# Banded attention scores: the low key parts in zero-padded tiles of full height

## Chip, cores and metric

The kernel runs on one NeuronCore of a Trainium2 chip. The metric is the device time of one execution in microseconds (us). The engines are named as in the profile: PE is TensorE's matrix multiply and PEld its weight load, DVE is VectorE, ACT is ScalarE, POOL is GpSimd, SP issues most DMAs.

## The reference, cut to what matters

One layer of a bidirectional hybrid encoder over 512 tokens of width 1024: a state space branch and a windowed attention branch side by side, a gated merge, cross attention to 256 memory rows, a feed-forward block. All is float32. The change lies in the windowed attention. It has 16 query heads of 64 features over 4 key heads; a block of 128 queries sees the key block before it, its own and the one after it.

```python
def windowed_gqa_with_sink(q, k, v, sink):
    ...
    qb = q.reshape(b, nb, ATTN_BLOCK, ATTN_KV_HEADS, ATTN_GQA, ATTN_HEAD_DIM)
    kb = band_blocks(k)
    vb = band_blocks(v)
    scores = jnp.einsum('bnqhrd,bnkhd->bnhrqk', qb, kb).astype(jnp.float32) * (ATTN_HEAD_DIM ** -0.5)
    ...
    scores = jnp.where(valid[None, :, None, None], scores, -jnp.inf)
    ...
    probs = jax.nn.softmax(jnp.concatenate([scores, sink_col], axis=-1), axis=-1)[..., :-1]
    out = jnp.einsum('bnhrqk,bnkhd->bnqhrd', probs.astype(v.dtype), vb)
    return out.reshape(b, s, ATTN_WIDTH)
```

## The kernel before

**Exact products in two parts.** Every float32 operand of a large product is split into a high part of the narrower type float32r and a low part, the rest. A projection (`mac`, lines 138 to 140) is then three matmuls for each 128 rows of the contraction: high by high, low activations by high weights, high activations by low weights. Weights come in granules of 128 x 1024; `load` fetches one (`raw`), ACT or DVE casts the high part (`whi`, lines 126 and 128), DVE or POOL subtracts to get the low part (`wlo`, line 129). Granules are prepared two steps ahead, in three buffers.

**The scores.** A query head has 64 features, and the PE contracts over up to 128 rows. `q_step` puts a head's high parts in one half of the 128 rows of its tile `qs` and the low parts in the other half. `k_step` puts the high key parts twice, in both halves of `kd`. One matmul (line 772) of the whole `qs` tile with `kd` therefore gives high by high plus low by high. The product of the high query parts with the low key parts is added by a second matmul (line 774), which takes only the 64 rows of `qs` that hold the high parts, and the same 64 rows of `kl`. Of `kl` there is one slot per pair of key heads: the low parts of one head fill its upper 64 rows, those of the other its lower 64.

**A block of attention.** `soft(pr, qb, kk)` handles four query heads that share a key head, for 128 queries; there are 16 such blocks, numbered 0 to 15 in this text in the order of execution. With 2 or 3 key blocks in reach a score row has 256 columns (blocks 0, 1, 6 to 9, 14, 15) or 384. For each head there is a pair of matmuls (lines 772 and 774) into one of two PSUM banks `sa`, then DVE's reduction (line 776), which adds the mask, finds the maximum and so frees the bank. After four of them three small DVE operations make the exponent's bias `ngm` (lines 780 to 782), ACT takes four exponentials (line 785), DVE adds and inverts the sums (787, 788) and normalises the four tiles (line 790). `turn` transposes the probabilities on PE (line 800), ACT copies them out (line 802), `mix` multiplies them by the values (line 813), ACT and DVE split the result (817, 818). The tiles `sm` have two buffers for each head, so the reductions of a block wait for the transposes of the block two before it.

**What sets the order.** `weave` spreads the attention steps among projection steps, and the framework then orders the instructions of each engine by its own estimates when the kernel is built; each engine runs its own list strictly in order. PE's list has projection matmuls between the score pairs one by one.

Of the kernel before, what the change touches and what calls it, by code (L numbers as in the profile page):

```python
# [9 lines left out]
F32 = mybir.dt.float32  # L10
F32R = mybir.dt.float32r
AF = mybir.ActivationFunctionType
ALU = mybir.AluOpType
AX = mybir.AxisListType

P = 128
D = 1024
S = 512
KT = D // P
NCH = S // P  # L20
# [8 lines left out]

# columns of the packed constants  # L30
C_ID, C_ONE = 0, 128
C_TRF, C_TRB = 256, 384
C_COS, C_SIN, C_MASK = 512, 1024, 1536
C_N = 1920
# columns of the packed vectors
V_MIX, V_XAT, V_MEM, V_FFN, V_FIN = 0, 8, 16, 24, 32
V_CW, V_CB, V_SSD = 40, 160, 184
V_DTB, V_AL, V_DSK, V_SNK = 200, 201, 202, 218
V_N = 234
# granules of the input projection  # L40
G_DT, G_K, G_V, G_Q, G_GA, G_SSD, G_GS, G_N = 0, 1, 3, 5, 13, 21, 61, 69
# [24 lines left out]
def weave(a, b):  # L66
    """The steps of a and b in one list, both spread evenly over it."""
    key = [((i + 0.5) / len(a), 0, i) for i in range(len(a))] + [((i + 0.5) / len(b), 1, i) for i in range(len(b))]
    return [(a, b)[w][i] for _, w, i in sorted(key)]
# [3 lines left out]
def bidir_hybrid_layer(ctx: ExitStack, tc: tile.TileContext, io, dbg=None):  # L73
    nc = tc.nc
# [11 lines left out]
    x1 = xp.tile([P, KT, S], F32, tag="x1", name="x1")  # L86
# [14 lines left out]

# [1 line left out]
    vec = const.tile([P, V_N], F32, tag="vec", name="vec")  # L103
# [4 lines left out]
    half = const.tile([P, 4], F32, tag="half", name="half")  # L108
# [4 lines left out]

# [1 line left out]
    def load(spec, i):  # L115
# [30 lines left out]

# [1 line left out]
    def rms_stat(pool, sumsq, nchunk, width, eps):  # L148
# [38 lines left out]
    def gain_split(hi, lo, t, g):  # L187
        """hi + lo = t * g, exactly split."""
        nc.scalar.activation(hi, t, AF.Copy, scale=g)
        nc.vector.scalar_tensor_tensor(lo, t, g, hi.bitcast(F32), op0=ALU.mult, op1=ALU.subtract)  # L190

# [1 line left out]
    steps = []  # L193
    st = {}
# [19 lines left out]

    # ======================= keys and values of the memory =======================
    # (in buffers that the state space branch uses later)
    opens("mp")
# [62 lines left out]
    def load_x():  # L280
        p = st["mp"]
        st["hh"] = p.tile([P, KT, S], F32R, tag="hh", name="hh")
        st["hl"] = p.tile([P, KT, S], F32R, tag="hl", name="hl")
        for nm in ("nb", "wt", "dec"):
            st[nm] = p.tile([P, NCH, 64], F32, tag=nm, name=nm)
        st["xacc"] = st["sp"].tile([P, S], F32, tag="vrow", name="vrow")
# [40 lines left out]

    # ======================= state space branch =======================
    def ssd_open():
# [5 lines left out]

    # time steps: softplus, cumulative sums within chunks, decays
    # (x1 is free until the first group is projected: it holds the intermediate values)
    def dt_step(w):
# [147 lines left out]
    def group_scan(g):  # L486
        # what each chunk receives from the chunks before (after) it
        def weigh(d, n):
# [21 lines left out]

        # cumulative decays of one head, both directions, the same row on every partition
        def rows(h):
# [39 lines left out]

        # within the chunks, two heads side by side: features of a head, by tokens
        def inner(i):
# [9 lines left out]

        # what arrives from other chunks, likewise
        def arrive(i):
# [20 lines left out]

        # gate with silu(z), kept doubled: the norm removes the factor
        def gate(i):
# [16 lines left out]
        nn, ar, ga, gs = ([w(i) for i in range(4)] for w in (inner, arrive, gather, gate))  # L606
        # stages of the heads: each stage some steps behind the one before
        order = []
# [34 lines left out]

    # first gates of this branch, while the last group is scanned
    def early_gate(m):
# [45 lines left out]

    # ======================= windowed attention =======================
    def at_open():
        p = st["at"]
        ca = p.tile([P, C_N - C_COS], F32, tag="ca", name="ca")
        nc.scalar.dma_start(ca, io["consts"][:, C_COS:C_N])
        st["ca"] = ca
        st["kd"] = p.tile([P, 4, S], F32R, tag="kd", name="kd")
        st["kl"] = p.tile([P, 2, S], F32R, tag="kl", name="kl")
        st["vt"] = p.tile([P, NCH, 256], F32, tag="vtok", name="vtok")  # L700
        st["oh"] = st["mo"].tile([P, KT, S], F32R, tag="oh", name="oh")
        st["ol"] = st["mo"].tile([P, KT, S], F32R, tag="ol", name="ol")
# [14 lines left out]
    def k_step(i):  # L717
        def f(w):
            t = rope(w)
            kd, kl = st["kd"], st["kl"]  # L720
            for kk in range(2):
                own, oth = slice(64 * kk, 64 * kk + 64), slice(64 - 64 * kk, 128 - 64 * kk)
                nc.scalar.copy(kd[own, 2 * i + kk], t[own])
                nc.scalar.copy(kd[oth, 2 * i + kk], t[own])
                nc.vector.tensor_tensor(kl[own, i], t[own], kd[own, 2 * i + kk].bitcast(F32), op=ALU.subtract)
        return f
# [17 lines left out]

    # q of one head: high parts over 64 partitions, low parts over the other 64
    def q_step(i):
# [13 lines left out]
    def soft(pr, qb, kk):  # L760
        def f():
            aw = st["at"]
            b0, b1 = blocks(qb)
            n = (b1 - b0) * P
            m0 = 2 * S + (b0 - qb + 1) * P
            own = slice(64 * kk, 64 * kk + 64)
            sm = [aw.tile([P, 384], F32, tag=f"sm{r}", name=f"sm{r}", bufs=2) for r in range(4)]
            mx, ngm, es, dn = (aw.tile([P, 4], F32, tag=t, name=t, bufs=2) for t in ("mx", "ngm", "es", "dn"))
            for r in range(4):
                sp = bank("sa")  # L770
                qs = st["qs", 4 * pr + r, kk]
                nc.tensor.matmul(sp[:, :n], qs[:, qb * P:(qb + 1) * P], st["kd"][:, 2 * pr + kk, b0 * P:b1 * P],  # L772
                                 start=True, stop=False)
                nc.tensor.matmul(sp[:, :n], qs[own, qb * P:(qb + 1) * P], st["kl"][own, pr, b0 * P:b1 * P],  # L774
                                 start=False, stop=True)
                nc.vector.tensor_tensor_reduce(
                    out=sm[r][:, :n], in0=sp[:, :n], in1=st["ca"][:, m0:m0 + n],
                    scale=1.0, scalar=-3.0e38, op0=ALU.add, op1=ALU.max, accum_out=mx[:, r:r + 1])
            snk = vec[:, V_SNK + 8 * pr + 4 * kk:V_SNK + 8 * pr + 4 * kk + 4]
            nc.vector.scalar_tensor_tensor(ngm, mx, 0.125, snk, op0=ALU.mult, op1=ALU.max)  # L780
            nc.vector.tensor_tensor(es, snk, ngm, op=ALU.subtract)
            nc.vector.tensor_scalar(ngm, ngm, -1.0, None, op0=ALU.mult)
            nc.scalar.activation(es, es, AF.Exp)
            for r in range(4):
                nc.scalar.activation(sm[r][:, :n], sm[r][:, :n], AF.Exp, bias=ngm[:, r:r + 1], scale=0.125,
                                     accum_out=dn[:, r:r + 1])
            nc.vector.tensor_tensor(dn, dn, es, op=ALU.add)
            nc.vector.reciprocal(dn, dn)
            for r in range(4):
                nc.vector.tensor_scalar(sm[r][:, :n], sm[r][:, :n], dn[:, r:r + 1], None, op0=ALU.mult)  # L790
            st["sm", kk] = sm
        return f
# [61 lines left out]

    # ======================= merge and output projection =======================
    def gate_a(m):
# [16 lines left out]

    # new residual tile, its split for the next projection, its square
    def residual(m, old, acc, gbase, sq):
# [27 lines left out]

    # ======================= cross attention =======================
    opens("xa")

    # keys and values of one head, split
    def kv_part(h):
# [104 lines left out]

    # ======================= feed forward =======================
    opens("ff")
# [43 lines left out]

    # last output tile and final norm, one half of the tokens after the other  # L1060
    def ff_last(*ws):
# [52 lines left out]

# [1 line left out]
    specs = [g for _, gr in steps for g in gr]  # L1116
# [26 lines left out]
def _gran(w):  # L1143
    """[K, M] -> [M/128, 128, K]: per output tile, the K tiles side by side."""
    k, m = w.shape
    return np.ascontiguousarray(w.reshape(k // P, P, m // P, P).transpose(2, 1, 0, 3)).reshape(m // P, P, k)
# [74 lines left out]
```

## Time and profile before

| | |
|---|---|
| median of 3 runs | 1351.72 us (1351.01 to 1351.82) |
| span of the profiled execution | 1350.6 us |
| PE busy | 1284.6 us, 95% of the span |
| DVE busy | 812.4 us, 60% |
| ACT busy | 580.8 us, 43% |
| first score matmul to the last | 604.0 to 725.5 us |

The profile gives the profiled execution by its span, from the first to the last instruction; its own time is not listed apart. The runs are timed from outside and lie 0.4 to 1.2 us above that span. Matmuls are pipelined and their listed ends are modelled: a PE that is listed as busy can still be waiting between two matmuls, so the starts of successive matmuls say what one costs.

### The profile page before, as it was taken

What the parts mean: (1) busy time and instruction counts of PE and PEld (TensorE: products, weight loads), DVE (VectorE), ACT (ScalarE), POOL (GpSimd) and SP (SyncE); (2) the same over time, 40 slices, a digit from 0 to 9 for tenths busy, and PEclk for the clock granted to TensorE, in tenths of its full rate; (3) what the DMA queues carried; (4) which work ended last, traced back from release to release, by engine and by line L of the source; (5) the groups of instructions that cost most, each with busy time, mean ns of one, the idle gap of its engine ahead of it and who ended that gap; (6) DMA issues with size and microseconds to landing.
All of it is one profiled execution on the core that took longest, in us unless ns stands there. A gap on an engine that the chain in (4) does not pass through costs nothing.

```text
span 1350.6 us, 16359 instructions
## 1 busy us (share of the span) xinstructions
PE 1284.6 (95%) x6084; PEld 1022.9 (76%) x6084; DVE 812.4 (60%) x1355; ACT 580.8 (43%) x1001; POOL 316.5 (23%) x259
## 2 busy tenths in 40 slices
PE   6889998998999999999999999999999999999996
PEld 5667776776777678876656888888888888888886
DVE  5797788788679776577765444566443444333323
ACT  6437376257256253256855333444332332222221
POOL 3344254234453562320000001100211111110001
PEclk9999999998999999999999999999999999999998
DMA  7435344243223323321102332411323322233331
GB/s 244 129 102 160 112 143 129 74 125 125 69 94 119 109 74 99 115 80 46 47 16 85 118 94 94 156 63 49 101 88 105 96 94 94 96 102 90 99 98 63
DMA packets 45440, 134.95 MB, mean 100 GB/s; under 512 B 5104, under 2 KB 8560, under 8 KB 45360
## 3 DMA queue, kind: packets, MB, share of 16 engines
q1 hardware_dynamic: 43072, 129.77, 30.4%
q10 hardware_dynamic: 1584, 2.03, 0.5%
q0 software_dynamic: 704, 2.10, 0.4%
q8 instruction: 48, 0.79, 0.2%
q14 instruction: 32, 0.26, 0.1%
HBM read 129.55 MB, written 4.33 MB: 99 GB/s over the span
## 4 chain that ended last, share of the span: by engine, by line
PE 69%; DVE 12%; issue 6%; POOL 6%; ACT 4%; DMA 2%; SPq 0%; DVEq 0%; POOLq 0%; ACTq 0%
PE mm L138 19%; PE mm L140 19%; PE mm L139 19%; DVE cvu L411 2%; DVE rt L538 2%; DVE wlo L129 2%; PE sa L774 2%; PE sb L813 2%; PE sb L800 1%; POOL mt L545 1%; POOL vv L585 1%; PE sa L772 1%; PE sb L986 1%; ACT whi L128 1%; PE sb L500 1%
## 5 line engine op out<-in xcount | busy, mean ns | idle before, releaser
L138 PE MATMUL mm<-hh,whi 128*128 128x512 f32 x968 | 388.4, 401 | 8.8 <-DVE cvu L411 5.4
L128 ACT CAST whi<-raw 128x1024 fp32r<-128x1024 f32 (+2 forms) x192 | 199.0, 1037 | 454.4 <-PE mm L139 394.0
L140 PE MATMUL mm<-hh,wlo 128*128 128x512 f32 x968 | 383.5, 397 | 0.9 <-DVE wlo L129 0.8
L139 PE MATMUL mm<-hl,whi 128*128 128x512 f32 x968 | 382.5, 395 | 0.2 <-DVE hl L310 0.2
L129 DVE TENSOR_TENSOR wlo<-raw,whi 128x1024 fp32r<-128x1024 f32 (+2 forms) x193 | 242.4, 1257 | 127.4 <-ACT whi L128 121.1
L138 PEld LDWEIGHTS mm<-hh,whi 128*128 128x128 f32 x968 | 184.8, 191 | 52.1 <-issue 10.3
L140 PEld LDWEIGHTS mm<-hh,wlo 128*128 128x128 f32 x968 | 184.2, 190 | 43.1 <-issue 2.3
L139 PEld LDWEIGHTS mm<-hl,whi 128*128 128x128 f32 x968 | 184.5, 191 | 39.0 <-issue 1.6
L185 POOL TENSOR_TENSOR sq_acc<-sq_acc,sq 128x512 f32<-128x512 f32 x14 | 24.8, 1771 | 276.4 <-ACT sq L184 276.4
L1039 POOL TENSOR_TENSOR fa<-fa,row 128x512 f32<-128x512 f32 x22 | 39.1, 1779 | 192.3 <-ACT fa L1038 192.3
L411 DVE SCALAR_TENSOR_TENSOR cvu<-mm,hcw,cvu 128x510 f32<-128x510 f32 (+1 forms) x96 | 70.9, 739 | 5.9 <-ACT cvu L408 5.5
L138 PE MATMUL mm<-fh,whi 128*128 128x512 f32 (+1 forms) x198 | 72.4, 366 | 0.0
L139 PE MATMUL mm<-fl,whi 128*128 128x512 f32 (+1 forms) x198 | 72.4, 365 | 0.0
L140 PE MATMUL mm<-fh,wlo 128*128 128x512 f32 (+1 forms) x198 | 72.4, 365 | 0.0
L138 PE MATMUL mm<-vh,whi 128*128 128x512 f32 (+1 forms) x192 | 71.5, 373 | 0.0
L140 PE MATMUL mm<-vh,wlo 128*128 128x512 f32 (+1 forms) x192 | 69.3, 361 | 0.0
L139 PE MATMUL mm<-vl,whi 128*128 128x512 f32 (+1 forms) x192 | 68.8, 358 | 0.0
L538 DVE TENSOR_SCALAR rt<-rt,nb 128x128 f32<-128x128 f32 x128 | 52.5, 466 | 20.9 <-POOL rt L530 17.5
L545 POOL TENSOR_TENSOR mt<-rt 128x512 f32<-128x512 f32 x32 | 48.0, 1503 | 71.8 <-ACT rt L539 33.8
L1041 DVE TENSOR_TENSOR ft<-fa,mm 128x512 f32<-128x512 f32 x22 | 15.1, 688 | 72.8 <-PE mm L140 70.7
L528 ACT ACTIVATE ear<-rt 64x1024 f32<-64x1024 f32 x32 | 33.9, 1060 | 55.7 <-POOL vv L585 51.9
L140 PE MATMUL mm<-oh,wlo 128*128 128x512 f32 x128 | 50.2, 392 | 0.0
(233 smaller groups left out, 2070.3 us busy)
## 6 DMA issues: line engine op xcount, KB each, us to landing
raw<-in_w_in SPq DMA_DIRECT2D x69, 512.0 KB, 3.5
raw<-in_w_fi SPq DMA_DIRECT2D x44, 512.0 KB, 3.5
rt<-adr SPq DMA_DIRECT2D x64, 256.0 KB, 4.3
raw<-in_w_bs SPq DMA_DIRECT2D x16, 512.0 KB, 3.4
raw<-in_w_fo SPq DMA_DIRECT2D x16, 512.0 KB, 3.5
raw<-in_w_xk SPq DMA_DIRECT2D x8, 512.0 KB, 3.8
raw<-in_w_ba SPq DMA_DIRECT2D x8, 512.0 KB, 3.4
raw<-in_w_mo SPq DMA_DIRECT2D x8, 512.0 KB, 3.5
```

What stands on the lines that cost most here:

```text
L128: nc.scalar.copy(hi[:, t], raw[:, t])
L129: (nc.gpsimd if i in LO_POOL else nc.vector).tensor_tensor(lo[:, t], raw[:, t], hi[:, t].bitcast(F32), op=ALU.subtract)
L138: nc.tensor.matmul(acc, wh, xh[:, k0 + k], start=first and k == 0, stop=False)
L139: nc.tensor.matmul(acc, wh, xl[:, k0 + k], start=False, stop=False)
L140: nc.tensor.matmul(acc, wl, xh[:, k0 + k], start=False, stop=last and k == nk - 1)
L411: nc.vector.scalar_tensor_tensor(u[:, b], acc[:, a], w5[j], u[:, b], op0=ALU.mult, op1=ALU.add)
L528: nc.scalar.activation(st["ear", h // 2][own], rt[own], AF.Exp)
L538: nc.vector.tensor_scalar(r, r, st["nb"][:, c, e0:e0 + 1], None, op0=ALU.add)
L545: nc.gpsimd.tensor_tensor(mt, st["rt", g, h][:, 0], st["rt", g, h][:, 1], op=ALU.add)
L774: nc.tensor.matmul(sp[:, :n], qs[own, qb * P:(qb + 1) * P], st["kl"][own, pr, b0 * P:b1 * P], start=False, stop=True)
L813: nc.tensor.matmul(av[64 * kk:64 * kk + 64], st["vt"][:, b0 + j, h * 64:(h + 1) * 64], st["pt", kk, j], start=j == 0, stop=j == b1 - b0 - 1)
L1039: nc.gpsimd.tensor_tensor(a, a, st["row2"], op=ALU.mult)
```

## The change

The low key parts get one slot for each key head, of 128 rows. The 64 rows that hold no low parts are set to zero once, when the attention buffers are opened, by four DVE memsets. The second score matmul then takes the whole `qs` tile, the same weights as the first one, and the padded `kl`: the low query parts meet zeros. The small tiles `nb`, `wt` and `dec` of the state space branch move to the pool that is closed before the attention opens, which gives the room for the larger `kl`. Comments and blank lines go as well, which isn't shown.

```diff
@@ load_x @@
         for nm in ("nb", "wt", "dec"):
-            st[nm] = p.tile([P, NCH, 64], F32, tag=nm, name=nm)
+            st[nm] = st["sp"].tile([P, NCH, 64], F32, tag=nm, name=nm)
@@ at_open @@
-        st["kl"] = p.tile([P, 2, S], F32R, tag="kl", name="kl")
+        st["kl"] = p.tile([P, 4, S], F32R, tag="kl", name="kl")
+        for kh in range(4):
+            oth = slice(64 - 64 * (kh % 2), 128 - 64 * (kh % 2))
+            nc.vector.memset(st["kl"][oth, kh].bitcast(F32), 0.0)
@@ k_step @@
-                nc.vector.tensor_tensor(kl[own, i], t[own], kd[own, 2 * i + kk].bitcast(F32), op=ALU.subtract)
+                nc.vector.tensor_tensor(kl[own, 2 * i + kk], t[own], kd[own, 2 * i + kk].bitcast(F32), op=ALU.subtract)
@@ soft @@
-            own = slice(64 * kk, 64 * kk + 64)
...
-                nc.tensor.matmul(sp[:, :n], qs[own, qb * P:(qb + 1) * P], st["kl"][own, pr, b0 * P:b1 * P],
+                nc.tensor.matmul(sp[:, :n], qs[:, qb * P:(qb + 1) * P], st["kl"][:, 2 * pr + kk, b0 * P:b1 * P],
                                  start=False, stop=True)
```

On DVE the four memsets stand where the last products of the state space branch are handed over (`cvt` is its product with the norm's row, line 639) and the weights of the attention's projections are prepared. Before, this part of DVE's list was:

```order
L639 TENSOR_TENSOR cvt<-mm,vrow 128x512 [waits PE_49,Pool_49]
L129 TENSOR_TENSOR wlo<-raw,whi 128x1024 [waits DVE_49]
L126 CAST whi<-raw 128x1024 [waits DMAHW5_49,PE_49]
L129 TENSOR_TENSOR wlo<-raw,whi 128x1024 [waits DVE_49,PE_49]
L126 CAST whi<-raw 128x1024 [waits DMAHW7_49,PE_49]
```

With the change, at the same place:

```order
L639 TENSOR_TENSOR cvt<-mm,vrow 128x512 [waits PE_49,Pool_49]
L129 TENSOR_TENSOR wlo<-raw,whi 128x1024 [waits DVE_49]
L702 MEMSET kl 64x512 [waits DMASW3_49,DMASW2_49,Pool_49]
L702 MEMSET kl 64x512 x3
L126 CAST whi<-raw 128x1024 [waits DMAHW5_49,PE_49]
L129 TENSOR_TENSOR wlo<-raw,whi 128x1024 [waits DVE_49,PE_49]
```

The memsets go in ahead of a weight cast, and the first of them takes over a wait for POOL and for two old DMA queues that stood on the first copy into `vtok` eight rows further down. Nothing else moves on any engine: PE's list has the same 5489 rows in the same order. In the changed kernel the lines from 700 on have higher numbers: by three up to line 765, then by two (the score matmuls are lines 774 and 776 there).

## Rows read from the trace of the kernel before

**Rows 1.** Page, part 2: DVE's busy tenths and PE's granted clock, 40 slices.

```profile
DVE  5797788788679776577765444566443444333323
PEclk9999999998999999999999999999999999999998
```

**Rows 2.** Windows: us, busy of PE, PEld, DVE, ACT, POOL; PEclk, DMA share, GB/s.

```profile
604.00:620.00 16.00, 14.82 (x46) 9.31 (x46) 9.94 (x34) 6.25 (x21) 0.00 (x0) 0.79 0.20 67
620.00:680.00 60.00, 59.95 (x268) 37.41 (x266) 45.61 (x136) 46.64 (x109) 5.16 (x4) 1.00 0.13 45
680.00:737.00 57.00, 57.00 (x250) 33.16 (x249) 34.46 (x141) 34.01 (x99) 0.00 (x0) 1.00 0.05 19
```

**Rows 3.** PE timeline, pair of 384 columns: start, us, line, names, rows*columns, operands.

```profile
640.04 0.34 PE L772 MATMUL sa<-kd,qs 128*128 128x384 f32 x1
640.31 0.44 PE L774 MATMUL sa<-kl,qs 64*128 64x384 f32 x1
640.68 0.50 PE L140 MATMUL mm<-hh,wlo 128*128 128x512 f32 x1
641.01 0.40 PE L138 MATMUL mm<-hh,whi 128*128 128x512 f32 x1
641.25 0.39 PE L139 MATMUL mm<-hl,whi 128*128 128x512 f32 x1
```

**Rows 4.** Timeline of PE, a pair of 256 columns.

```profile
684.04 0.28 PE L772 MATMUL sa<-kd,qs 128*128 128x256 f32 x1
684.25 0.38 PE L774 MATMUL sa<-kl,qs 64*128 64x256 f32 x1
684.56 0.50 PE L140 MATMUL mm<-hh,wlo 128*128 128x512 f32 x1
684.89 0.28 PE L772 MATMUL sa<-kd,qs 128*128 128x256 f32 x1
```

**Rows 5.** Timeline of PEld, the weight loads of the matmuls in rows 3.

```profile
640.30 0.18 PEld L774 LDWEIGHTS sa<-kl,qs 64*128 64x128 f32 x1 [0.31 <-issue]
640.78 0.19 PEld L138 LDWEIGHTS mm<-hh,whi 128*128 128x128 f32 x1
```

**Rows 6.** Timeline of PE in the cross attention, scores of full height, 256 columns.

```profile
893.57 0.28 PE L955 MATMUL sa<-kvl,qh 128*128 128x256 f32 x1
893.68 0.28 PE L955 MATMUL sa<-kvh,ql 128*128 128x256 f32 x1
```

**Rows 7.** Waits from 604 to 737: who for whom, us in total, times, longest.

```profile
DVE sm L776 <- PE sa L774: 19.8, 29, 3.8
PEld sa L774 <- issue: 15.5, 55, 0.8
```

**Rows 8.** Timeline of PE: the third score pair of block 0.

```profile
607.32 0.58 PE L772 MATMUL sa<-kd,qs 128*128 128x256 f32 x1 [1.18 <-DVE mx L776]
```

**Rows 9.** Timeline of POOL and DVE where the memsets go in.

```profile
551.34 2.20 POOL L640 TENSOR_TENSOR x<-x,cvt 128x512 f32<-128x512 f32 x1 [1.23 <-DVE cvt L639]
554.39 0.69 DVE L126 CAST whi<-raw 128x1024 fp32r<-128x1024 f32 x1 [2.00 <-PE mm L139]
559.83 0.69 DVE L126 CAST whi<-raw 128x1024 fp32r<-128x1024 f32 x1 [3.42 <-PE mm L139]
```

**Rows 10.** Timeline of PE and DVE: transposes and normalisations of blocks 9 to 11.

```profile
693.88 1.09 PE L800 MATMUL sb<-cst,sm 128*128 128x128 f32 x8
697.39 0.44 PE L772 MATMUL sa<-kd,qs 128*128 128x384 f32 x1
700.26 1.41 DVE L790 TENSOR_SCALAR sm<-sm,dn 128x384 f32<-128x384 f32 x4
701.87 0.60 PE L800 MATMUL sb<-cst,sm 128*128 128x128 f32 x4
705.70 1.41 DVE L790 TENSOR_SCALAR sm<-sm,dn 128x384 f32<-128x384 f32 x4
707.06 1.53 PE L800 MATMUL sb<-cst,sm 128*128 128x128 f32 x12
```

## The prediction

> **What bounds the kernel now.** The page came first, then the waits and the windows of the stretch in which the scores are computed, then the timelines of PE and PEld there. From 604 to 737 us PE is listed as busy nearly throughout, 59.95 of 60 us and 57.00 of 57 in the last two windows, while DVE and ACT are at three quarters, then at 60% [rows 2]. So PE sets the pace there, but part of what is listed as busy is waiting, and the starts show it. Projection matmuls of 512 columns follow each other every 0.24 us (641.01 to 641.25). Around a score pair they don't: from 772 to 774 it is 0.27, from 774 to the next projection 0.37, and from that one to the next 0.33 [rows 3]. The weight load of 774 starts at 640.30, when the matmul before it is over, whereas the load for line 138 starts at 640.78, 0.10 after the matmul that it lies beside had started [rows 5]. The one thing that sets 774 apart is its form, 64*128 beside 128*128 on both sides. The waits name it in total: 15.5 us in which the load of 774 waited for nothing but issue, and 19.8 us in which DVE's reductions waited for 774 [rows 7]. I read this as PE emptying at each change of form, once into and once out of each of the 64 second matmuls.
>
> **What the change is worth on PE.** It makes the second matmul 128*128 too. Nothing is taken away: 64 pairs stay 64 pairs, the weight load grows from 64 to 128 rows and the columns streamed are the same.
> A pair of 256 columns and the projection after it take 0.85 now (684.04 to 684.89) [rows 4]. Scores of full height and 256 columns follow each other at 0.11 [rows 6]; I take 0.12, so the same three matmuls should take 0.12 + 0.12 + 0.24 = 0.48: 0.37 less. For 384 columns no matmul of full height stands between two of its kind in the trace. Halfway between 0.12 and 0.24 is 0.18, so 0.97 now (640.04 to 641.01) [rows 3] becomes 0.18 + 0.18 + 0.24 = 0.60, also 0.37 less. If 384 columns cost as much as 512, it is 0.97 - 0.72 = 0.25. I take 0.37 for all 64 pairs: **23.7 us is the ceiling**, 32 x 0.37 + 32 x 0.25 = 19.8 with the dear wide pairs. That the full height costs nothing by itself is read from the same rows, whose matmuls are all of full height.
>
> **What of it arrives.** PE runs its list in order, and the list stays as it is, so where PE gets ahead it meets results that aren't there yet. Three parts.
> First, 604 to 620, 9 pairs. The first two bring nothing: PE then waited 1.18 us for DVE to free a bank [rows 8] and will only wait longer. The other seven are worth 2.6; I take 2.2.
> Second, 620 to 680, 26 pairs, ceiling 9.6 us. ACT needs 46.64 and DVE 45.61 of these 60 us [rows 2]; in 50.4 us ACT would be busy for 93%. Only one of the 40 slices has DVE, the busier of the two over the span, at nine tenths [rows 1]; where an engine is fed and emptied by others, in order, it doesn't fill up. At 85% these 46.64 us take 54.9. That leaves 5.1.
> Third, 680 to 737, 29 pairs, ceiling 10.7 us. DVE and ACT have room here (34.46 and 34.01 us, 75% of what would be left), so I follow one turn of the loop from block to block [rows 10]. From 697.39, the third pair of block 11, PE has four pairs and five projections until the transposes of block 10 at 701.87. Without the emptying that is 4 x 0.37 = 1.48 less. The normalisation that the transposes need started at 700.26, 1.61 before them, and its last tile is wanted by the fourth transpose. It stands in DVE's list behind the reductions of block 11's last pairs, which come at least one pair sooner, 0.37. So it would be at 699.89, PE there at 700.39: the 1.48 arrive, and nearly all the slack is gone. From there to the transposes of block 11 at 707.06 PE has three more pairs, 1.11, together 2.59. Their normalisation began at 705.70 and lasts 1.41. It stands behind a reduction of block 12 whose pair comes after the transposes of block 10, so it moves by 1.48 and some 0.2 of that pair, to 704.0, and its fourth tile ends at 705.4. PE would be there at 704.5, does the first transposes and then waits about half a microsecond. So some 2.1 of 2.59 arrive, 80%. That turn begins with slack that is gone afterwards, and the second part comes out at 53%; I take 65% for the whole third part: 7.0.
> Sum: 2.2 + 5.1 + 7.0 = **14.3 us**.
>
> **The rest of the edits.** The four memsets are a form that the trace doesn't have. Each writes 512 elements per row; the cast of twice as many takes 0.69 us [rows 9], so I bound one by 0 and 0.69 and take 0.5, 2 us for four. The first waits for POOL's last addition, 551.34 + 2.20 = 553.54, so the cast that stood at 554.39 comes at about 555.6, 1.2 us late, and with the upper bound at 553.54 + 2.76 = 556.30, 1.9 late. Behind it are that granule's low part and the next casts. DVE had 3.42 us without work ahead of the cast at 559.83 [rows 9], which takes the delay up, and weights are prepared two granules ahead. I cost it at nothing; without that cover it would be 1.9 us. The wait for POOL moves from a copy eight rows further down to the memset and ends before it would matter. The three small tiles only change their pool. After 737 the same list follows, and DMA has room in these windows (shares of 0.20, 0.13 and 0.05) [rows 2], so what is gained in the attention stays.
>
> **The forecast.** The profiled span is 1350.6 us, the median 1351.72, 1.1 above it. 1350.6 - 14.3 = 1336.3 for the span, 1337.4 for the median. Less than 0.2%, 2.7 us, is about what a measurement of this kernel can't tell from no change.
>
> **Rivals.**
> *All of it arrives.* The waits that I put in are mine, and DVE's 19.8 us of waiting for 774 say that its own work moves up with PE. Against it: the slack of 1.61 at block 10 is used up by four pairs. It gives 1351.7 - 23.7 = 1328.0. Chance 0.15.
> *DVE and ACT already set the pace.* If the loop of reduction, exponential and normalisation doesn't move with PE, only the slack at one set of transposes can be won, 1.6 us: 1350.1. Against it stand the 19.8 us of rows 7. Chance 0.06.
> *The wait isn't due to the form.* The load of 774 could start late because it goes to rows of the array that the matmul before it is using. Then a second load of full height, onto all of them, starts as late as now, the pair keeps its 0.97 and the time stays at 1351.7. Against it: the load for line 138 is of full height and starts beside a matmul of full height [rows 5]. Chance 0.04. The Trainium skill, "TensorE: Matmul & The Clock Gate", Part 3, "The mechanism", says in its list of what overlaps that weight loads overlap with matmuls in flight only where their row groups differ. By that rule the gain is nothing; the trace does not agree, with 0.10 us from the start of the matmul to that of the load beside it.
> *Slower: the clock falls.* PE's granted clock fell after the wait of 1.18 us at 607 [rows 8], and was 0.79 on average from 604 to 620 [rows 2]: 16 x 0.21 = 3.4 us of PE's full-speed time. A PE that runs ahead waits at each block's transposes, and if the clock falls there as well, each fall costs up to 3.4 us. With five falls the 14.3 us are gone, with six it is slower: 1351.7 + 6 x 3.4 - 14.3 = 1357.8. Against it: from 620 to 737 the clock stayed at 1.00 [rows 2] although PE emptied twice for each pair, and the waits that I expect are about half a microsecond. Chance 0.04.
>
> **How the numbers follow.** The forecast has what is left, 0.71, and reaches from 1331 (80% in all three parts) to 1345 (a third of the ceiling). Below it lies the ceiling's 1328. I let the range go from 1328 to 1345; left out are the three others, 0.14, and some 0.05 below it. Faster by over 0.2%: 0.71 + 0.15 and a little of the second rival, 0.88. Within 0.2%: 0.09. Slower: 0.03, the clock's fall being mostly a smaller gain.
>
> **What would show it.** In the trace after, both score matmuls have the form 128*128, the load of the second one starts beside the first, and its wait of 15.5 us for issue is all but gone. From the first matmul of a pair to the second it is 0.12 at 256 columns and 0.18 at 384, and 0.24 from the projection behind a pair to the next. The score stretch, 604.0 to 725.5 now, ends about 13 us sooner. PE waits for DVE's normalisation at the transposes, in many pieces of half a microsecond or so, 8 to 10 us in all. The clock falls once at 607 as before. The casts at 554 are 1 to 2 us late and nothing else moves there. I am wrong if the starts around a pair stay as they are, if PE shows no new waits (then it is the ceiling), or if the clock falls again between 620 and 725.

## The result, and the profile after

The changed kernel takes **1330.63 us** (median of 4 runs, 1327.94 to 1331.93) against 1351.37 (4 runs beside it): ratio 0.9842, 95% interval 0.9828 to 0.9856, 20.7 us less. In a later comparison it took 1333.51 against 1351.34, ratio 0.986 (0.9838 to 0.9882), 17.8 less. The forecast was 1337.4, its range 1328 to 1345. The profiled execution of the changed kernel has a span of 1330.2 us, 20.4 below the one before. In the changed kernel line 774 is the first score matmul, 776 the second, 778 the reduction, 792 the normalisation, 802 the transposes, 815 the products with the values.

The timeline of PE answers to [rows 3, 4]. First a pair of 256 columns with the projection behind it, then one of 384:

```profile
611.28 0.28 PE L774 MATMUL sa<-kd,qs 128*128 128x256 f32 x1
611.40 0.28 PE L776 MATMUL sa<-kl,qs 128*128 128x256 f32 x1
611.52 0.40 PE L140 MATMUL mm<-hh,wlo 128*128 128x512 f32 x1
611.76 0.28 PE L774 MATMUL sa<-kd,qs 128*128 128x256 f32 x1
...
617.11 0.33 PE L774 MATMUL sa<-kd,qs 128*128 128x384 f32 x1
617.28 0.34 PE L776 MATMUL sa<-kl,qs 128*128 128x384 f32 x1
617.45 0.39 PE L138 MATMUL mm<-hh,whi 128*128 128x512 f32 x1
617.68 0.40 PE L139 MATMUL mm<-hl,whi 128*128 128x512 f32 x1
```

Read the starts. At 256 columns it is 0.12, 0.12, 0.24: 0.48 in place of 0.85. At 384 it is 0.17, 0.17, 0.23: 0.57 in place of 0.97. The saving is 0.37 and 0.40 a pair, so the ceiling is 32 x 0.37 + 32 x 0.40 = 24.6 us.

The timeline of PEld answers to [rows 5]: the load of the second score matmul now starts at 617.11, at the same moment as the first matmul that it lies beside, and not when that one is over.

```profile
617.11 0.19 PEld L776 LDWEIGHTS sa<-kl,qs 128*128 128x128 f32 x1
617.28 0.19 PEld L138 LDWEIGHTS mm<-hh,whi 128*128 128x128 f32 x1
```

The windows of the score stretch, with the columns of [rows 2]:

```profile
604.00:620.00 16.00, 14.10 (x76) 11.23 (x75) 14.34 (x49) 10.39 (x29) 0.65 (x1) 1.00 0.23 77
620.00:667.00 47.00, 46.11 (x236) 32.23 (x238) 40.26 (x122) 42.50 (x102) 4.59 (x4) 1.00 0.15 46
667.00:717.00 50.00, 50.00 (x260) 33.05 (x259) 34.83 (x145) 34.54 (x101) 0.00 (x0) 1.00 0.09 32
```

ACT is now busy for 42.50 of 47 us in the middle window, 90%, where it was at 78%, and DVE for 14.34 of 16 us in the first, 90% too. PE has openly idle time in the first two. The waits of the stretch, 604 to 737, answer to [rows 7]:

```profile
DVE sm L778 <- PE sa L776: 6.9, 9, 2.4
PEld sa L774 <- DVE mx L778: 6.8, 18, 2.3
PE sa L774 <- DVE mx L778: 2.3, 2, 1.9
PEld sa L776 <- issue: 1.6, 2, 0.8
PEld sb L802 <- ACT pt L804: 0.9, 3, 0.4
PE sb L802 <- DVE sm L792: 0.2, 1, 0.2
```

The second matmul's wait for issue went from 15.5 us to 1.6 and DVE's wait for it from 19.8 to 6.9. What is new is waiting until DVE has read a score bank. Before, the view had these two lines for it:

```profile
PEld sa L772 <- DVE mx L776: 2.3, 4, 1.6
PE sa L772 <- DVE mx L776: 1.2, 1, 1.2
```

The lines of PE and PEld can't be added up. At the third pair the matmul (idle for 1.88 us) and its weight load (idle for 2.3) wait for the same bank at the same time; only the load's line holds all of them, 6.8 us in place of 2.3. PE's wait for the normalisation at the transposes is listed with 0.2 us.

The third score pair [rows 8] waits longer than before, and the memsets [rows 9] stand where the order put them:

```profile
608.64 0.39 PE L774 MATMUL sa<-kd,qs 128*128 128x256 f32 x1 [1.88 <-DVE mx L778]
...
549.39 0.69 DVE L639 TENSOR_TENSOR cvt<-mm,vrow 128x512 f32<-128x512 f32 x1 [1.17 <-POOL x L640]
...
555.05 2.37 DVE L702 MEMSET kl<- 64x512 f32 x4 [1.32 <-POOL x L640]
557.35 0.62 DVE L126 CAST whi<-raw 128x1024 fp32r<-128x1024 f32 x1
...
561.22 0.69 DVE L126 CAST whi<-raw 128x1024 fp32r<-128x1024 f32 x1 [1.92 <-PE mm L139]
```

One turn of the loop near the end, the blocks of [rows 10]: the third pair of block 11, the normalisation and the transposes of block 10, then those of block 11.

```profile
682.54 0.44 PE L774 MATMUL sa<-kd,qs 128*128 128x384 f32 x1
...
684.96 1.41 DVE L792 TENSOR_SCALAR sm<-sm,dn 128x384 f32<-128x384 f32 x4
685.55 0.65 PE L802 MATMUL sb<-cst,sm 128*128 128x128 f32 x4
...
689.25 1.40 DVE L792 TENSOR_SCALAR sm<-sm,dn 128x384 f32<-128x384 f32 x4
689.84 1.41 PE L802 MATMUL sb<-cst,sm 128*128 128x128 f32 x11
```

The normalisation starts 0.59 before its transposes both times, where the lead was 1.61 and 1.36. The slack is smaller and PE barely waits.

**Where the time went.** The trace's starts cut the stretch from the first score matmul to the last product with the values into the prediction's three parts: up to the 10th score pair, from there to the 36th, and the rest. The time from that last product to the last matmul of the kernel is 606.9 to 607.1 us in every kernel of this table, so what is gained in the attention stays. "Clock" is the mean granted clock in the 16 us from the first score matmul, as in the first of [rows 2]; 1.00 is 2.4 GHz, and a fall goes to 0.50, 1.2 GHz. The kernels e1 to e11 are described below. One execution of e5 took 1600.13 us, at a mean granted clock of 0.745; it is in no ratio and no row here.

| kernel | pairs of full height | clock | part 1 | part 2 | part 3 | in all |
|---|---|---|---|---|---|---|
| before | 0 | 0.79 | 16.38 | 60.13 | 55.29 | 131.79 |
| e1, before again | 0 | 0.89 | 14.94 | 60.14 | 55.31 | 130.39 |
| e2 | 0 | 0.79 | 16.34 | 60.13 | 55.31 | 131.78 |
| after | 64 | 1.00 | 11.01 | 53.07 | 45.77 | 109.86 |
| e9, after again | 64 | 0.89 | 12.57 | 53.09 | 45.75 | 111.41 |
| e4 | 64 | 1.00 | 11.02 | 53.07 | 45.75 | 109.85 |
| e3 | 32 | 1.00 | 12.32 | 56.36 | 50.67 | 119.36 |
| e10 | 56 | 0.89 | 14.61 | 53.74 | 45.76 | 114.12 |

Without a fall of the clock there is no execution of the kernel before, so the pair to compare is e1 with e9, both at 0.89: 130.39 - 111.41 = **19.0 us**, in parts 2.4, 7.05 and 9.55. These are one execution each. From the median before, 1351.4 - 19.0 = 1332.4, which lies between the two medians measured after.

Of the ceiling, 24.6 - 19.0 = 5.6 us did not arrive. The starts of the matmuls, before and after, show where PE loses them. It stands still ahead of first score matmuls: 2.0 us at the third pair, where it was 1.3, and 0.7 in all at two pairs of block 4, where it didn't before. At the transposes the starts sum to 1.4 us more, 0.8 between transposes and 0.6 on the way into them. And in 27 of the 62 pairs whose two matmuls stand side by side the load of the first score matmul comes late, at most 0.04 us ahead of its matmul: these pairs take 0.18 to 0.22 (256 columns) or 0.26 to 0.28 (384) from their first matmul to the second, in place of 0.12 and 0.17, together 2.6 us. That is about what is missing, but some of the late loads were late before as well, and no run separates the three.

### The profile page after: what moved, and what is told of

It reads as the page before. It is cut to its first block, busy times and chain, and to the rows that moved or that the text cites. A ratio compares the mean times of both kernels' runs of the same rounds, so it can differ in the third digit from the quotient of the medians.

```text
span 1330.2 us, 16362 instructions
## 1 busy us (share of the span) xinstructions
PE 1259.6 (95%) x6084; PEld 1016.9 (76%) x6084; DVE 811.2 (61%) x1359; ACT 579.1 (44%) x1001; POOL 316.4 (24%) x259
## 4 chain that ended last, share of the span: by engine, by line
PE 62%; DVE 12%; issue 10%; POOL 7%; ACT 5%; DMA 2%; SPq 0%; DVEq 0%; POOLq 0%; ACTq 0%
PE mm L138 18%; PE mm L139 18%; PE mm L140 18%; DVE rt L538 2%; DVE cvu L411 2%; DVE wlo L129 2%; POOL vv L585 1%; PE sb L815 1%; POOL mt L545 1%; ACT whi L128 1%; PE sb L802 1%; DMA rt<-adr 1%; POOL rsw L714 1%; POOL rt L530 1%; PE sb L988 1%
## 5 line engine op out<-in xcount | busy, mean ns | idle before, releaser
L545 POOL TENSOR_TENSOR mt<-rt 128x512 f32<-128x512 f32 x32 | 47.7, 1493 | 72.1 <-ACT rt L539 34.1
L139 PE MATMUL mm<-ol,whi 128*128 128x512 f32 x128 | 50.0, 391 | 0.0
```

Source lines behind the costliest of these rows:

```text
L139: nc.tensor.matmul(acc, wh, xl[:, k0 + k], start=False, stop=False)
L545: nc.gpsimd.tensor_tensor(mt, st["rt", g, h][:, 0], st["rt", g, h][:, 1], op=ALU.add)
```

## Experiments

The theory: PE empties whenever a matmul of 64 rows follows or precedes one of 128, so the gain goes with the number of such changes. Rivals: the padded tiles, their places or the order of DVE's list do it; a weight load has to wait for the matmul ahead of it whatever the forms; DVE and ACT limit what arrives; the clock does part of it.

**e1, the kernel before once more.** No edit.

> The kernel before, profiled once more. The trace of the kernel after shows no fall of PE's granted clock at the first scores, where the trace of before had 6.8 us at 0.50. If the fall belongs to the kernel before (its PE empties at each pair there), it stands again within a few us of the first scores, and the mean clock from the first pair to 16 us later is about 0.8. If it is an accident of one execution, it can be missing here, with a clock of 1.00 there, and the span is some 3 us shorter than 1350.6.

1348.62 us, one run, span 1346.8. Two of the three parts repeat to 0.02 us; the first is 1.44 shorter, with the clock at 0.89 in place of 0.79. So parts 2 and 3 can be compared to a few hundredths, and part 1 apart from that fall, whose length differs from one execution to the next.

**e2, padded tiles, but 64 rows.** The changed kernel with its memsets, its larger `kl` and the moved small tiles; only the second matmul takes the half-height slices as before.

```diff
+                own = slice(64 * kk, 64 * kk + 64)
-                nc.tensor.matmul(sp[:, :n], qs[:, qb * P:(qb + 1) * P], st["kl"][:, 2 * pr + kk, b0 * P:b1 * P],
+                nc.tensor.matmul(sp[:, :n], qs[own, qb * P:(qb + 1) * P], st["kl"][own, 2 * pr + kk, b0 * P:b1 * P],
```

> The kernel after, with its padded tiles, its memsets and its moved small tiles, but the second score matmul takes the 64 rows that hold low parts, as before. If the gain comes from the form of the matmul alone, this runs like the kernel before, 1351 us within 2.5, with 0.27 and 0.37 us around a pair of 384 columns. If the new places of the tiles or the memsets have a part in it, it lies clearly between the two kernels, below 1347.

1352.24 us (12 runs), ratio 0.9995 (0.9983 to 1.0006): no difference, and the three parts of before to 0.04 us. All of the gain comes from the height of the second matmul.

**e3, half the dose.** The changed kernel, but in the blocks of the odd key heads (kk = 1) the second matmul takes 64 rows. PE's list is in the same order.

```diff
+                rows = slice(0, P) if kk == 0 else slice(64, P)
-                nc.tensor.matmul(sp[:, :n], qs[:, qb * P:(qb + 1) * P], st["kl"][:, 2 * pr + kk, b0 * P:b1 * P],
+                nc.tensor.matmul(sp[:, :n], qs[rows, qb * P:(qb + 1) * P], st["kl"][rows, 2 * pr + kk, b0 * P:b1 * P],
```

> The kernel after, but in every second block of attention (32 of the 64 pairs) the second score matmul takes 64 rows as before; PE's list has the same order. If each pair that changes its form has its own price and PE sets the pace, half of the gain of 20.7 us is left: 1341 us, 1339 to 1343. If DVE and ACT begin to set the pace part of the way, the first half of the pairs brings more than the second: 1335 to 1338. If the gain came from something that has to be gone altogether, such as the clock, it stays at 1347 or above.

1339.62 us (6 runs), ratio 0.9911 (0.9893 to 0.9929). The stretch is 119.36, 9.5 more than after, both at full clock: half the pairs cost half of the 19.0. In parts 2 and 3 it stands half way too, 56.36 between 60.13 and 53.07 and 50.67 between 55.29 and 45.77. So up to the full dose the gain did not flatten: DVE and ACT did not begin to set the pace part of the way. PE's timeline shows both kinds in one kernel (777 is the second matmul here), first a block of 64 rows, then one of 128:

```profile
676.98 0.28 PE L774 MATMUL sa<-kd,qs 128*128 128x256 f32 x1
677.19 0.38 PE L777 MATMUL sa<-kl,qs 64*128 64x256 f32 x1
677.50 0.50 PE L138 MATMUL mm<-hh,whi 128*128 128x512 f32 x1
677.85 0.34 PE L774 MATMUL sa<-kd,qs 128*128 128x384 f32 x1
678.03 0.34 PE L777 MATMUL sa<-kl,qs 128*128 128x384 f32 x1
678.20 0.39 PE L139 MATMUL mm<-hl,whi 128*128 128x512 f32 x1
```

0.21 and 0.31 ahead of and behind a matmul of 64 rows and 256 columns; 0.18 and 0.17 for the larger 384 columns where all are of 128 rows.

**e5, the second matmul cut into two halves of columns.** The kernel before; the 64-row product is made by two matmuls of half the columns, so 128 loads in place of 64, each of 64 rows, the second behind a matmul of its own form.

```diff
-                nc.tensor.matmul(sp[:, :n], qs[own, qb * P:(qb + 1) * P], st["kl"][own, pr, b0 * P:b1 * P],
-                                 start=False, stop=True)
+                for c0, c1 in ((0, n // 2), (n // 2, n)):
+                    nc.tensor.matmul(sp[:, c0:c1], qs[own, qb * P:(qb + 1) * P],
+                                     st["kl"][own, pr, b0 * P + c0:b0 * P + c1], start=False, stop=c1 == n)
```

> The kernel before with the second score matmul cut into two of half the columns each: same 64 rows, same weights, same form, one after the other, so that for the first time a matmul of 64*128 follows one of 64*128. If it is the change of form at which PE empties, the second half's load starts beside the first half, the two halves follow each other at about their columns' time (0.06 to 0.12 us for 128 columns, 0.09 to 0.12 for 192), and the pair with the projection behind it takes its 0.85 and 0.97 us, 0.05 more at most. If a half-height weight load always waits for the matmul before it, whatever the form, there are 0.2 us or more between the halves and the pair is longer by 0.15 to 0.25: 64 pairs make that 10 to 16 us in all, 1361 us or more. The order on PE differs a little from before, so the time itself is only a rough sign.

Ratio 1.0151 (1.0126 to 1.0175), 1368.67 to 1375.33 us. By the time alone this is what was expected if each load waits, 1361 us or more; but PE's order had changed, and the starts decide. For them the same kernel was run again.

> The kernel with the second score matmul cut into two halves of its columns once more, for a trace at the clock of the others. As before: if PE empties at a change of form, the loads of the two halves start about 0.1 us apart, the second beside the first half's matmul, and from the first half to the matmul behind the pair it is 0.37 us at 384 columns as for the undivided one, 0.45 at most. If each half-height load waits for the matmul before it, the two loads are 0.2 us or more apart and it is 0.55 or more.

1369.83 us, span 1367.7, clock 0.973. PE's and PEld's timelines (775 is the second matmul, x2 its two halves):

```profile
652.30 0.30 PEld L775 LDWEIGHTS sa<-kl,qs 64*128 64x128 f32 x2 [0.19 <-issue]
652.30 0.46 PE L775 MATMUL sa<-kl,qs 64*128 64x192 f32 x2
652.69 0.44 PE L772 MATMUL sa<-kd,qs 128*128 128x384 f32 x1
...
658.81 0.44 PE L775 MATMUL sa<-kl,qs 64*128 64x128 f32 x2
659.18 0.38 PE L772 MATMUL sa<-kd,qs 128*128 128x256 f32 x1
```

Both halves together take 0.39 at 384 columns and 0.37 at 256, against 0.37 and 0.31 undivided [rows 3, 4]. The two loads of 0.19 each lie within 0.30, so the second starts 0.11 after the first, and only the first waits for issue. A second load onto the rows in use thus costs 0.02 to 0.06 and no new emptying: the wait belongs to the change of form, and the load rival falls. The 18 us by which the whole kernel is longer come from elsewhere. The build put PE's list in another order, which moves 43 projection matmuls from the stretch to behind it, and in the stretch the clock fell five times, for 34.1 us in all at 0.50. An estimate from these rows: the falls cost up to 34.1 / 2 = 17 us and the second loads 1 to 4, which is enough. No run separates them, and why the clock fell so often is open.

**e6 and e7, one PSUM bank more for the scores.** If the waits for score banks are what is missing of the ceiling, a third bank should bring it. It is taken from the transposes (e6) or from the projections (e7).

```diff
-        return ps.tile([P, 512], F32, tag=tag, name=tag, bufs={"mm": 3, "sa": 2, "sb": 3}[tag])
+        return ps.tile([P, 512], F32, tag=tag, name=tag, bufs={"mm": 3, "sa": 3, "sb": 2}[tag])
```

```diff
-        return ps.tile([P, 512], F32, tag=tag, name=tag, bufs={"mm": 3, "sa": 2, "sb": 3}[tag])
+        return ps.tile([P, 512], F32, tag=tag, name=tag, bufs={"mm": 2, "sa": 3, "sb": 3}[tag])
```

> The kernel after with three PSUM banks for scores and two instead of three for transposes and mixes. In the trace of after PE waits 9.1 us for DVE's reductions to free a score bank. If these waits are what keeps the rest of the ceiling back, they fall to 4 us or less and the time goes to 1324 to 1327 us. If the two remaining banks for transposes, mixes and the state space branch's sums take over, it stays within 2.5 us of 1330.6 or gets slower, 1333 and more, with new waits of PE for ACT's copies.

> The kernel after with three PSUM banks for scores and two instead of three for projections. Same reasoning: 1324 to 1327 us if the score banks are the limit in the attention and two projection banks are enough elsewhere. As projections make up most of the program and their results are read by DVE in several steps in the state space branch, a loss there is the rival: 1340 us or more.

e6: 1326.95 us, ratio 0.982 (0.9803 to 0.9836). e7: 1357.7, ratio 1.0043 (1.0027 to 1.006). The first score matmul starts at 625.4: the stages ahead of it, whose projections now have a bank less, take some 20 us more, and the stages behind the last product with the values 10 more (617.0 in place of 607.1). Its score stretch is the shortest of all, 106.0, but has 8 projection matmuls fewer. e6 moves 16 projection matmuls into the stretch, so its 111.35 can't be set beside 109.86 either. From the first score matmul to the last matmul of the kernel it takes 715.2, and after 717.0: 1.8 us of the difference are in the attention and behind it.

**e8, two low weight parts on POOL.** If DVE limited what arrives, two subtractions less should help.

```diff
-LO_POOL = range(10, 19)
+LO_POOL = (*range(10, 19), 88, 89)
```

> The kernel after, but the low parts of the two weight granules that DVE prepares while the first scores come in (indices 88 and 89) are made by POOL, which has nothing to do there. In the trace of after PE waits 1.88 us at the third pair of the first block for DVE, which does one of these subtractions (1.23 us) and a gate first, and the other one two reductions later. If that queue is the whole wait, it falls to about 0.7 us and the time by 1 to 3 us, to 1328 to 1330. If PE meets the next limit at once, or POOL's subtraction is late for the projection, it stays within 1 us of 1330.6 or gets slower.

1333.45 us, ratio 0.9871 (0.9851 to 0.9891), the stretch 113.4 in place of 109.9. The wait at the third pair did fall, from 1.88 us to 0.56, but the time did not: parts 1 and 2 are longer, 11.87 and 55.75 in place of 11.01 and 53.07. POOL takes 5.49 us for the two, DVE 1.22 for one, which may be what was lost; how much DVE's load matters isn't tested cleanly by it.

**e9, e10, e11, e4, in one comparison.** e9 is the changed kernel again, e11 is e6 again. e10 takes 64 rows in blocks 0 and 1 alone:

```diff
+                own = slice(64 * kk, 64 * kk + 64) if pr == 0 and qb == 0 else slice(0, P)
-                nc.tensor.matmul(sp[:, :n], qs[:, qb * P:(qb + 1) * P], st["kl"][:, 2 * pr + kk, b0 * P:b1 * P],
+                nc.tensor.matmul(sp[:, :n], qs[own, qb * P:(qb + 1) * P], st["kl"][own, 2 * pr + kk, b0 * P:b1 * P],
```

and e4 clears the tiles on POOL:

```diff
-            nc.vector.memset(st["kl"][oth, kh].bitcast(F32), 0.0)
+            nc.gpsimd.memset(st["kl"][oth, kh].bitcast(F32), 0.0)
```

> The changed kernel once more, beside the other three runs of this call. The score stretch, first score matmul to last product with the values, should again last 109 to 111 us without a fall of the granted clock in it, and the time should be 1329 to 1332 us. If the fall at 607 were a matter of chance in either kernel, it would show up here in one of two executions.

> The changed kernel, but the second score matmul of blocks 0 and 1, 8 of the 64 pairs, takes 64 rows as before. Theory (the emptying of PE in these first pairs, together with the wait for DVE, is what made the clock fall at 607): the granted clock goes to 0.50 near 607 for 3.4 or 6.8 us and the kernel loses 8 pairs at about 0.3, 2.3 us, and 1.7 to 3.4 more: 1334.5 to 1336.5 us. Rival (the fall has nothing to do with these pairs): no fall there, 2.3 us alone, or less where DVE's wait hides it: 1331.5 to 1333 us.

> The changed kernel with three PSUM banks for the scores and two for the transposes, beside the changed kernel of the same call. Theory (PE's waits for a free score bank, 9.1 us in the changed kernel, are part of what did not arrive of the ceiling): 1326 to 1328 us, 3 to 4 below the changed kernel, and the PE waits for DVE's mx stay under 4 us. Rival (the 1327 us seen came from the stretches ahead of the scores, where the clock happened to fall less): no difference beyond 1 us beside the changed kernel.

> The changed kernel with the four memsets issued on POOL in place of DVE. Theory (the memsets on DVE are covered by DVE's idle time behind them and cost nothing): the same time within 2.5 us, 1328 to 1333 us. Rival (the cast that comes late behind the memsets holds up the weights of a projection): 1.5 to 2 us faster than the changed kernel beside it.

*e9:* 1333.51 us, where 1329 to 1332 were expected. The clock did fall this time, behind the same wait that in the first profile of this kernel had left it at 1.00. PE's timeline and the windows of e9:

```profile
607.82 0.53 PE L774 MATMUL sa<-kd,qs 128*128 128x256 f32 x1 [1.88 <-DVE mx L778]
...
607.00:611.00 4.00, 3.18 (x10) 2.70 (x11) 3.70 (x12) 0.60 (x1) 0.00 (x0) 0.61 0.58 168
```

It cost 12.57 - 11.01 = 1.56 us in part 1 and nothing elsewhere. So a missing fall is not something that the change brings for certain.

*e10:* 1336.79 us, ratio 0.9887 (0.9869 to 0.9905). The clock fell as in e9, and the stretch is 114.12 - 111.41 = 2.71 longer. Of these, 2.04 lie in part 1: 8 pairs at 0.37 are 3.0, but PE stands still for 0.76 less at the third pair, so that the first two pairs cost nothing, as the prediction had it. The other 0.65 lie in part 2, where all pairs are of full height in both kernels: there PE comes to the transposes of a block whose normalisation isn't done, as its waits show (803 are the transposes here, 793 the normalisation).

```profile
PEld sb L803 <- DVE sm L793: 0.9, 1, 0.9
```

Of the fall it decides nothing, since e9 had one too.

*e11:* 1328.42 us, ratio 0.983 (0.9813 to 0.9846), 5.1 below e9; the intervals of the two ratios overlap a little. From the first score matmul to the last matmul it is 715.0, in e9 718.4, of which 1.56 are the fall: 1.9 us remain, as with e6 (1.8). The waits of its stretch:

```profile
PE sa L774 <- DVE mx L778: 2.0, 1, 2.0
PEld sa L774 <- DVE mx L778: 1.6, 4, 0.8
PEld sb L802 <- ACT pt L804: 3.6, 10, 0.9
```

The waits for score banks fell from 6.8 to at most 3.6, both lines together. But the transposes, with a bank less, now wait 3.6 for ACT's copies (0.9 before). So part of what is missing of the ceiling goes with the banks, as the theory has it, though 2 us of it and not the 3 to 4 expected; PE's list, which the build reordered, changed with them. Where the rest of the 3.7 and 5.1 us by which the medians differ lies is open: the profiled execution of e6 starts its scores earlier than after's (602.3 against 605.7), but that of e11 later than e9's (605.9 against 604.8). With both measurements below the changed kernel's, this is the fastest version found.

*e4:* 1333.13 us beside 1333.51, and the three parts of after to 0.02 us. The memsets on DVE cost nothing.

## Why the prediction was right, and where its sizes were off

**A price at each change of form: shown.** e2 gives back the whole gain by the height alone, e3 half of it by half the pairs, e5 adds matmuls and loads of the same form at next to nothing. That PE empties there is the reading that fits the late loads; the profile doesn't show it as such. The prediction says that the load of 774 starts when the matmul ahead of it is over; by its listed, modelled end that matmul still has 0.08 us to go (640.04 + 0.34 against 640.30). The Trainium skill, "TensorEngine Tiling (Array Packing)", "Key Properties", says that changing the tiling mode drains TensorE; the trace agrees, with 0.37 to 0.40 us for the way in and out.

**The price.** 0.37 at 256 columns was exact, where the first load is early. At 384 it is 0.40: the pair takes 0.57 and not 0.60. The ceiling is 24.6, not 23.7.

**What arrives: the term that was too small.** 14.3 was forecast, 19.0 came, 77% of the ceiling. The first part was right, 2.2 against 2.4, and e10 bears out that the first two pairs bring nothing. The second was 5.1 against 7.05: ACT's 46.64 us fill 88% of the 53.09 that are left, where 85% was taken. The assumption was three points too low, and each is worth about 0.6 us; that ACT's share is what sets this part was assumed, and no run tests it. The row that it was taken from is also misread: two of DVE's 40 slices stand at nine tenths, not one [rows 1]. The third was 7.0 against 9.55, and there the cut from 80% to 65% is the step that failed. The turn that was followed by hand came out as worked out up to the transposes of block 10: from the third pair of block 11 to them 3.01 us where 4.48 were before, 1.47 won and 1.48 forecast. To the transposes of block 11 it is 4.29 and was 5.19, 0.90 won where about 0.6 were allowed: 2.37 of 2.59, 92%. The whole third part kept 9.55 of the 10.7 it was given as ceiling, 89%, or 85% of 11.2 with the dearer wide pairs. The turn had been typical, and there was no row for cutting it further. (Up to the first of these transposes PE has six projections, not five; no sum uses that.)

**The range.** 80% in all three parts gives 1332.7 to 1333.4, and a third of the ceiling 1343.8; the 1331 and 1345 that stand for them lie 1 to 2 us further out. 1330.63 is below 1331 too, so it falls inside only because the lower end was taken down to the ceiling's 1328. The stretch, with 19.0 us where 14.3 were forecast, is the better measure of how far off the sizes were.

**Where PE waits: wrong place.** 8 to 10 us at the transposes were forecast. The starts of successive transposes sum to only 0.84 us more than before, and the steps from a projection to the first of them to 0.56 more. Normalisation moves up nearly as fast as PE, because the reductions that it stands behind are fed by PE. What PE meets instead is a score bank that DVE hasn't read: the loads' waits for it are 6.8 us where 2.3 were before; e6 and e11 take about half of that away and win 2 us.

**The clock falls once at 607 as before: open.** It fell in all four profiles of this order of PE's list in which the pairs of blocks 0 and 1 have 64 rows (before, e1, e2, e10). With all 128 rows there, and the same banks, it fell in e9 and not in after, e4 and e8; nor did it in e3, where only block 0 is of full height. That points to fewer falls after the change, worth 1.5 to 3 us each time, but with one or a few executions of each kernel and e9 among them it isn't certain, and what decides it was not found. It did not fall again between 620 and 717 in after, so the slower rival did not happen.

**Memsets and casts: right.** One memset took 0.485 us (0.5 was taken). The cast behind them came 7.96 us after the start of line 639's product, in e4 without memsets on DVE 6.38, so 1.6 late (1.2 forecast, 1.9 at most). The next cast came 11.83 and 11.82 after it: DVE's idle time took the delay up.

**The rivals.** All of it arrives, 1328.0: with 23.7 us it has 4.7 too much, as the forecast's 14.3 has 4.7 too little; to 1330.63 the rival is nearer, to 1333.51 the forecast. DVE and ACT set the pace, 1350.1: refuted by the straight line from 0 over 32 to 64 pairs. A load that must wait for the rows in use: refuted by the load of 776, which starts together with a matmul on all 128 rows (617.11), and by e5. The list in the Trainium skill, "TensorE: Matmul & The Clock Gate", Part 3, "The mechanism", by which weight loads overlap only where row groups differ, would have given no gain; the measurement decides here: loads of full height started beside matmuls of full height. A rival that nobody named, that the second matmul gains by taking the same weights as the first, is answered by [rows 6], where two matmuls of full height with different weights follow each other at 0.11.

## What to carry to other kernels

A short matmul whose contraction uses half of the rows, alone among matmuls of full height, can cost more than its own streaming: look at the starts of its neighbours, not at its busy time, and try padding the other operand with zeros. When estimating how much of a gain on one engine arrives, follow a turn of the loop by hand and don't cut what it gives without a row that says so (here the turn was nearer than the cut); engines that are fed by the faster one move up with it. Once PE is ahead, the number of banks between it and its reader is the next thing to look at, and a bank taken from elsewhere has to be paid for there. Don't add the waits of PE and PEld in one view: they can be the same wait.

## What was not expected of the hardware

Not every extra cost around a pair is gone. Behind transposes, a pair of 384 columns still takes 0.26 from its first matmul to the second in place of 0.17, though all are of 128 x 128, as the timeline of PE after shows:

```profile
615.73 1.18 PE L802 MATMUL sb<-cst,sm 128*128 128x128 f32 x8
616.67 0.42 PE L774 MATMUL sa<-kd,qs 128*128 128x384 f32 x1
616.93 0.34 PE L776 MATMUL sa<-kl,qs 128*128 128x384 f32 x1
```

No run tests the cause, but PEld's timeline says what goes with it. The load of that first matmul starts at 616.64, 0.03 ahead of its matmul; that of the next pair, which takes 0.17, starts at 616.95, 0.16 ahead of 617.11:

```profile
616.64 0.19 PEld L774 LDWEIGHTS sa<-kd,qs 128*128 128x128 f32 x1
616.95 0.19 PEld L774 LDWEIGHTS sa<-kd,qs 128*128 128x128 f32 x1
```

It is so for all 62 pairs: the 27 whose first load is late by this measure are the slow ones, whatever stands ahead of them, and the 34 whose load is 0.11 or more ahead take 0.11 to 0.12 and 0.17 to 0.18 (one lies between, 0.07 and 0.16). The 0.17 of the rows above is therefore what a pair costs when its first load could go early, and not what every pair costs.

And executions of one PE list differ ahead of the scores: the first score matmul starts at 604.3, 602.0 and 605.5 us in before, e1 and e2, where nothing on PE differs, while parts 2 and 3 repeat to a few hundredths. Much of the spread of 3 to 6 us between single runs can come from there; comparing one stretch from trace to trace tells tenths of a microsecond that the medians can't.
